# Sorting a unit's matmuls into a block of wide and a block of narrow ones

## The chip, the core and the metric

The program runs on one core of a Trainium2 chip. The metric is the device time of one execution in microseconds (us); lower is better. The chip's TensorE (PE in the profile) multiplies a stationary 128x128 block, loaded by an instruction of its own (PEld), with a moving operand of up to 512 columns and adds the product into PSUM. ScalarE (ACT), VectorE (DVE) and GpSimd (POOL) do the rest; SyncE (SP) issues most transfers.

## The reference, cut to what matters

Two transformer blocks over 256 tokens of width 2048. Block one: a gated convolution module, then a feed-forward part with a squared ReLU. Block two: stick-breaking and forgetting attention, 8 heads each, then another such feed-forward part. Everything is float32. The change touches the products that the reference writes as

```python
h @ w_up                                       # both feed-forward parts, 2048 -> 8192
proj = jnp.einsum('bsd,de->bse', h, w_in[l])   # of it the columns of q and k
```

## The kernel before, in words

**Hi and lo.** A float32 weight is split into `hi` (rounded to the matmul's fp32r format, by ACT, line 127) and `lo = raw - hi` (DVE, line 128). Activations are split in the same way; `xt[:, k, 0, :]` is the high half of 128 input columns for all 256 tokens, `xt[:, k, 1, :]` the low half. A product is the sum of hi·hi, hi·lo and lo·hi.

**Units.** All weights go through one list of steps. A unit is a piece of 512x512 weights (1 MB), loaded by SP into one of three `raw` buffers, split into one of three `hi` and one of three `lo` buffers, and used by one function. `emit` splits two units ahead (`SPLITS`) and loads three further ahead (`LOADS`), so the cast for unit i+2 is emitted before the matmuls of unit i; its buffers are those of unit i-1.

**The unit with stationary weights** (`ws_unit`, used by `up`, lines 614 to 632, and by q and k in `proj`). The weight block `wh` or `wl` is stationary. It holds 4 output blocks m by 4 input blocks k. For each (m, k) there is one wide matmul (`wh` with both halves of the activations, 512 columns, line 222) and one narrow matmul (`wl` with the high half alone, 256 columns, line 224, or 221 for the very last k). The two alternate, m outside and k inside. Four units kq = 0 to 3 add into the same four PSUM banks; they make a group of 64 wide and 64 narrow matmuls. Two PSUM tiles of two banks each, tag `ps2`, carry them: tile 0 for m = 0 and 1, tile 1 for m = 2 and 3. There are two `ps2` buffers in all.

**After kq = 3** each tile is read by an ACT copy and a DVE add (`u_t` line 626 and `u_z` line 628 for up; `q_t` lines 905 and 906 for q and k, where line 907 then writes `qk`). Only then may the next user of that tile start.

**The order around it.** Feed-forward: up(0), up(1), down(0), up(2), down(1) and so on; `down` is four units of `xs_unit`, in which the activations are stationary and every matmul is 512 wide (lines 231 to 233, tile `dn`, PSUM tag `ps1`). Mixer: for each of four groups of heads (two forgetting, two stick-breaking) v by `xs_unit` (tile `pv`, also `ps2`), q and k by `ws_unit` (tile `pj`), with the attention of the group before between the units: `z` products right after k, and `o` and `om` products between the next q units. After the first q comes the forget gate (`pf`). The first stage (tile `pw`, lines 518 to 521) uses 256-column matmuls only, each with its own load. From step 40 on, the instructions of each engine are ordered by the framework and not by hand.

Of the kernel before, what the change touches and what calls it, by code (L numbers as in the profile page):

```python
# [15 lines left out]
P = 128  # L16
T = 256
# [16 lines left out]
def kernel(  # L34
# [5 lines left out]
    x, out = x[0], out[0]  # L40
# [25 lines left out]

    state = {}

# [1 line left out]
    ident = const.tile([P, P], F32, name="ident")  # L70
    ones = const.tile([P, P], F32, name="ones")
    ones_c = const.tile([P, P], F32, name="ones_c")
# [17 lines left out]
        nc.scalar.dma_start(out=t, in_=bass.AP(tensor=v.tensor, offset=v.offset, ap=[[0, P], [1, D]]))  # L90
        return t

# [1 line left out]
    steps = []  # L94

    def unit_std(w, r0, c0):
# [76 lines left out]

    mm = nc.tensor.matmul

# [1 line left out]
    def split_act(src, hi, lo):  # L177
        nc.scalar.copy(hi, src)
        nc.vector.tensor_tensor(out=lo, in0=src, in1=hi.bitcast(F32), op=ALU.subtract)
# [31 lines left out]
    def new_ss(name):  # L211
        return small.tile([P, 2, 4], F32, tag="ss", name=name, bufs=2)

    def ws_unit(ps, hi, lo, xt, kq, m0=0, nm=4):
        for m in range(nm):
            for k in range(4):
                wh, wl = hi[:, k, m * P:(m + 1) * P], lo[:, k, m * P:(m + 1) * P]
                o = ps[m]
                last = kq == 3 and k == 3
                if last:  # L220
                    mm(o[:, 0:T], wl, xt[:, k, 0, :], start=False, stop=False, skip_group_check=True)
                mm(o, wh, xt[:, k, :, :], start=(kq == 0 and k == 0), stop=last)  # L222
                if not last:
                    mm(o[:, 0:T], wl, xt[:, k, 0, :], start=False, stop=False, skip_group_check=True)  # L224

    def xs_unit(ps, hi, lo, xt, first, last):
        for h in range(2):
# [4 lines left out]
                mm(ps[h], xh, lo[:, k, :], start=False, stop=False)  # L232
                mm(ps[h], xl, hi[:, k, :], start=False, stop=(last and k == 3))  # L233

# [1 line left out]
    s1 = ExitStack()  # L236
    p1 = s1.enter_context(tc.tile_pool(name="stage1", bufs=1))
    cpool = s1.enter_context(tc.tile_pool(name="cpool", bufs=4))
# [91 lines left out]
        for h in range(2):  # L330
            nc.gpsimd.tensor_tensor(out=res[:, h, :], in0=res[:, h, :], in1=rowbc, op=ALU.add)

# [1 line left out]
    xs_t = p1.tile([P, NB, T], F32, name="xs_t")  # L334
    u_t = [p1.tile([P, 2, T + 2 * PAD], F32, name=f"u{i}") for i in range(2)]
    acc0 = p1.tile([P, T], F32, name="acc0")
# [223 lines left out]
                            add_bias_rows()  # L560
                step(unit, fn)

# [1 line left out]
    def post_chunk(c, ss, gain, xts, delay):  # L564
        for h in range(2):
            sumsq(ss, h, c)

        def tr():
            xt = xt_tile("xn")
            for h in range(2):  # L570
                transpose_chunk(res[:, h, c * 512:(c + 1) * 512], h, c, gain, xt)
            xts.append(xt)
            if len(xts) == 4 and "after" in state:
                state.pop("after")()
        defer(delay, tr)
# [31 lines left out]
            srcs, _ = unit_std(w_pw2, q * 512, c * 512)  # L607
            step((srcs, "p" if q == 0 and c < 2 or (q, c) == (1, 0) else "v"), fn)

# [1 line left out]
    def ffn(w_u, w_d, tail):  # L611
        NG = FF // 512

        def up(g):
            for kq in range(4):
                def fn(hi, lo, kq=kq):
                    if kq == 0:
                        state["up"] = [ps2([P, 2, 512], f"up{i}") for i in range(2)]
                    pss = state["up"]
                    ws_unit([pss[m // 2][:, m % 2, :] for m in range(4)], hi, lo, state["xt"][kq], kq)  # L620
                    if kq == 3:
                        act = xt_tile("act")
                        for i in range(2):
                            ps = pss[i]
                            t = wk([P, 2, T], "u_t")
                            nc.scalar.copy(t, ps[:, :, T:2 * T])
                            z = wk([P, 2, T], "u_z")
                            nc.vector.tensor_tensor(out=z, in0=ps[:, :, 0:T], in1=t, op=ALU.add)
                            nc.vector.scalar_tensor_tensor(out=z, in0=z, scalar=0.0, in1=z, op0=ALU.max, op1=ALU.mult)
                            split_act(z, act[:, 2 * i:2 * i + 2, 0, :], act[:, 2 * i:2 * i + 2, 1, :])  # L630
                        state["act", g] = act
                step(unit_std(w_u, kq * 512, g * 512), fn)
# [59 lines left out]
            defer(2, spread)  # L692
        defer(1, rate)

# [1 line left out]
    s2 = ExitStack()  # L696

    def open_attention():
# [70 lines left out]
        state["lr"] = lr  # L769

    def attention(kind, grp, qk, v, mt):
        """Four heads: list of steps, each emitted in order with the projections between."""
        ap = state["ap"]
        qT, kT = qk
        per_pair = []
        for pair in range(2):
            st = {}
            heads = (2 * pair, 2 * pair + 1)
# [97 lines left out]
    def mixer():  # L876
        def proj(kind, grp, gi):
# [14 lines left out]
            for which in (0, 1):  # L892
                for kq in range(4):
                    def fn(hi, lo, kq=kq, which=which):
                        ap = state["ap"]
                        if kq == 0:
                            state["pj"] = [ps2([P, 2, 512], f"pj{i}") for i in range(2)]
                        pss = state["pj"]
                        ws_unit([pss[m // 2][:, m % 2, :] for m in range(4)], hi, lo, state["xt"][kq], kq)
                        if kq == 3:  # L900
                            dst = ap.tile([P, 4, T], F32, tag="qk", name=f"qk{which}", bufs=4)
                            rb = state["rb"][:, 1 - which:2 - which, :].to_broadcast([P, 2, T])
                            for i in range(2):
                                t = wk([P, 2, T], "q_t")
                                nc.scalar.copy(t, pss[i][:, :, T:2 * T])
                                nc.vector.tensor_tensor(out=t, in0=pss[i][:, :, 0:T], in1=t, op=ALU.add)  # L906
                                nc.vector.tensor_tensor(out=dst[:, 2 * i:2 * i + 2, :], in0=t, in1=rb, op=ALU.mult)
                            state["qk", gi, which] = dst
                            if which == 1:
                                mt = xt_tile("mt")  # L910
                                state["mt", gi] = mt
                                sts = attention(kind, grp, (state["qk", gi, 0], dst), state["v", gi], mt)
                                for n, s in enumerate(sts):
                                    defer(n + 1, s)
                    step(unit_std(w_in, kq * 512, base + 1024 * which + 512 * grp), fn)
                if gi == 0 and which == 0:
                    step(spread_gate, forget_gate)
# [54 lines left out]
                eng = nc.sync if j == 0 else nc.scalar  # L972
                eng.dma_start(out=out[h * P:(h + 1) * P, j * 1024:(j + 1) * 1024], in_=v)

# [1 line left out]
    for gi in range(len(groups)):  # L976
        stage1_group(gi)
    pw2()
# [54 lines left out]
```

## Time and profile before

| | |
|---|---|
| time, median of 3 runs | 2202.88 us (2202.71 to 2204.14) |
| span of the profiled execution, first to last instruction | 2200.8 us |
| PE busy | 2166.2 us, 98% of the span |
| DVE, ACT, POOL busy | 1436.8, 958.8, 175.2 us |
| mean granted TensorE clock | 0.996 of full speed |

The profiled execution has no time listed beside its span; the span is 2.1 us short of the median of the runs. "PE busy" counts modelled ends of pipelined matmuls, so the rate of a stream is read from start to start, not from the duration of one matmul.

### The profile page before, as it was taken

To read this page: it belongs to the slowest core of one execution; us is meant where nothing else is said; L and a number is where in the kernel's file an instruction comes from. 1 tells how busy PE (TensorE), PEld (TensorE's weight loads), DVE (VectorE), ACT (ScalarE), POOL (GpSimd) and SP (SyncE) were. 2 spreads that over 40 slices of the span, in tenths; PEclk is the share of its full clock that TensorE was granted. 3 is DMA by queue.
4 is the path that set the end of the run, shared out by engine and by line. 5 is a ranking of instruction groups with operands and counts; after the bars stand their busy time and mean duration, and the time that the engine had idled before them with its cause. 6 is when DMAs were issued, how large, how long until landed. Compare 5 with 4: busy or idle time off the path is not lost.

```text
span 2200.8 us, 27600 instructions
## 1 busy us (share of the span) xinstructions
PE 2166.2 (98%) x11521; PEld 1861.1 (85%) x11521; DVE 1436.8 (65%) x1648; ACT 958.8 (44%) x965; POOL 175.2 (8%) x88
## 2 busy tenths in 40 slices
PE   7999899999999999999999999999999999999998
PEld 7999778888888888888788888888888888888886
DVE  5997775666655666566866565676656665666656
ACT  6455454434333433343645454544333433343333
POOL 2886500000000000000000000000000000000000
PEclk9999999999999999999999999999999999999999
DMA  7555155555555555556544554455555555555553
GB/s 227 164 170 150 63 193 187 186 188 188 190 191 191 184 198 191 191 174 221 177 156 153 172 172 159 166 172 191 192 189 187 186 190 189 191 189 192 191 191 134
DMA packets 219612, 395.41 MB, mean 180 GB/s; under 512 B 8993, under 2 KB 46017, under 8 KB 219073
## 3 DMA queue, kind: packets, MB, share of 16 engines
q1 hardware_dynamic: 216160, 389.05, 54.6%
q10 hardware_dynamic: 2960, 4.27, 0.6%
q8 instruction: 90, 1.47, 0.3%
q0 software_dynamic: 368, 0.34, 0.1%
q14 instruction: 34, 0.28, 0.0%
HBM read 391.53 MB, written 2.10 MB: 179 GB/s over the span
## 4 chain that ended last, share of the span: by engine, by line
PE 97%; ACT 1%; DVE 1%; issue 0%; DMA 0%; ACTq 0%; SPq 0%; DVEq 0%
PE up L222 22%; PE dn L231 11%; PE dn L233 11%; PE dn L232 11%; PE up L224 10%; PE pj L222 5%; PE pj L224 3%; PE pw L521 2%; PE pw L518 2%; PE pw L520 2%; PE ca L386 2%; PE wo L232 1%; PE wo L233 1%; PE wo L231 1%; PE pv L233 1%; PE pv L231 1%
## 5 line engine op out<-in xcount | busy, mean ns | idle before, releaser
L128 DVE TENSOR_TENSOR lo<-raw,hi 128x2048 fp32r<-128x2048 f32 (+1 forms) x339 | 774.3, 2285 | 585.6 <-ACT hi L127 585.6
L127 ACT CAST hi<-raw 128x2048 fp32r<-128x2048 f32 (+1 forms) x369 | 702.8, 1906 | 935.9 <-PE up L222 340.3
L222 PE MATMUL up<-xn,hi 128*128 128x512 f32 x2048 | 718.3, 398 | 0.0
L224 PE MATMUL up<-xn,lo 128*128 128x256 f32 x1920 | 539.4, 281 | 0.0
L222 PEld LDWEIGHTS up<-xn,hi 128*128 128x128 f32 x2048 | 378.2, 188 | 83.8
L231 PE MATMUL dn<-hi,act 128*128 128x512 f32 x1024 | 398.8, 389 | 0.0
L233 PE MATMUL dn<-hi,act 128*128 128x512 f32 x1024 | 398.4, 389 | 0.0
L232 PE MATMUL dn<-lo,act 128*128 128x512 f32 x1024 | 398.3, 389 | 0.0
L224 PEld LDWEIGHTS up<-xn,lo 128*128 128x128 f32 x1920 | 362.5, 189 | 5.9
L641 DVE SCALAR_TENSOR_TENSOR res<-dn,rsq,res 128x512 f32<-128x512 f32 x256 | 191.4, 748 | 57.9 <-PE dn L233 57.9
L232 PEld LDWEIGHTS dn<-lo,act 128*128 128x128 f32 x1024 | 192.3, 188 | 40.1
L233 PEld LDWEIGHTS dn<-hi,act 128*128 128x128 f32 x1024 | 192.2, 188 | 40.1
L231 PEld LDWEIGHTS dn<-hi,act 128*128 128x128 f32 x1024 | 192.2, 188 | 38.6
L222 PE MATMUL pj<-xn,hi 128*128 128x512 f32 x512 | 179.7, 398 | 0.0
L394 DVE SCALAR_TENSOR_TENSOR acc<-u_p,wd,acc 128x256 f32<-128x256 f32 x385 | 151.6, 478 | 0.0
L128 POOL TENSOR_TENSOR lo<-raw,hi 128x2048 fp32r<-128x2048 f32 x30 | 138.5, 4620 | 85.6 <-ACT hi L127 85.6
L224 PE MATMUL pj<-xn,lo 128*128 128x256 f32 x480 | 134.5, 280 | 0.0
L518 PE MATMUL pw<-xa,hi 128*128 128x256 f32 x448 | 129.1, 288 | 0.7 <-ACT hi L127 0.7
L521 PE MATMUL pw<-xa,lo 128*128 128x256 f32 x448 | 127.6, 285 | 0.9 <-DVE lo L128 0.9
L520 PE MATMUL pw<-xa,hi 128*128 128x256 f32 x448 | 127.5, 285 | 0.0
L222 PEld LDWEIGHTS pj<-xn,hi 128*128 128x128 f32 x512 | 94.5, 188 | 20.6 <-DVE q_t L906 0.5
L224 PEld LDWEIGHTS pj<-xn,lo 128*128 128x128 f32 x480 | 90.6, 189 | 1.5
(259 smaller groups left out, 2033.5 us busy)
## 6 DMA issues: line engine op xcount, KB each, us to landing
raw<-in_ffn_w_up_dram SPq DMA_DIRECT2D x64, 1024.0 KB, 5.2
raw<-in_ffn_w_down_dram SPq DMA_DIRECT2D x64, 1024.0 KB, 5.1
raw<-in_w_up_dram SPq DMA_DIRECT2D x64, 1024.0 KB, 5.3
raw<-in_w_down_dram SPq DMA_DIRECT2D x64, 1024.0 KB, 5.0
raw<-in_w_in_dram SPq DMA_DIRECT2D x48, 1024.0 KB, 5.1
raw<-in_conv_w_pw_dram SPq DMA_DIRECT2D x64, 512.0 KB, 4.8
raw<-in_conv_w_pw_dram SPq DMA_DIRECT2D x16, 1024.0 KB, 5.1
raw<-in_w_out_dram SPq DMA_DIRECT2D x16, 1024.0 KB, 5.1
```

The source lines that it names most:

```text
L127: nc.scalar.copy(hi[:, j:j + n], raw[:, j:j + n])
L128: e.tensor_tensor(out=lo[:, j:j + n], in0=raw[:, j:j + n], in1=hi[:, j:j + n].bitcast(F32), op=ALU.subtract)
L222: mm(o, wh, xt[:, k, :, :], start=(kq == 0 and k == 0), stop=last)
L224: mm(o[:, 0:T], wl, xt[:, k, 0, :], start=False, stop=False, skip_group_check=True)
L231: mm(ps[h], xh, hi[:, k, :], start=(first and k == 0), stop=False)
L232: mm(ps[h], xh, lo[:, k, :], start=False, stop=False)
L233: mm(ps[h], xl, hi[:, k, :], start=False, stop=(last and k == 3))
L394: nc.vector.scalar_tensor_tensor(out=acc[k], in0=src, scalar=w, in1=acc[k], op0=ALU.mult, op1=ALU.add)
L518: mm(ps[:, m, :], wh, xt[:, k, 0, :], start=first and m % 2 == 0, stop=False, skip_group_check=True)
L520: mm(ps[:, m, :], wh, xt[:, k, 1, :], start=False, stop=False, skip_group_check=True)
L521: mm(ps[:, m, :], wl, xt[:, k, 0, :], start=False, stop=last, skip_group_check=True)
L641: nc.vector.scalar_tensor_tensor(out=r, in0=ps[h], scalar=state["rsq"][:, h:h + 1], in1=r, op0=ALU.mult, op1=ALU.add)
```

## The change

`ws_unit` issues the 16 wide matmuls of a unit in one block and the 16 narrow ones in another. For even kq the wide block comes first, for odd kq the narrow one, so that over a group the order is wide, narrow, narrow, wide, wide, narrow, narrow, wide. No matmul is added or taken away; the flags that begin and end an accumulation stay with the first and the last wide matmul of each m. The two unused parameters go. The rest of the diff takes out comments and a docstring.

```diff
-    def ws_unit(ps, hi, lo, xt, kq, m0=0, nm=4):
-        for m in range(nm):
-            for k in range(4):
-                wh, wl = hi[:, k, m * P:(m + 1) * P], lo[:, k, m * P:(m + 1) * P]
-                o = ps[m]
-                last = kq == 3 and k == 3
-                if last:
-                    mm(o[:, 0:T], wl, xt[:, k, 0, :], start=False, stop=False, skip_group_check=True)
-                mm(o, wh, xt[:, k, :, :], start=(kq == 0 and k == 0), stop=last)
-                if not last:
-                    mm(o[:, 0:T], wl, xt[:, k, 0, :], start=False, stop=False, skip_group_check=True)
+    def ws_unit(ps, hi, lo, xt, kq):
+
+        def wide():
+            for m in range(4):
+                for k in range(4):
+                    mm(ps[m], hi[:, k, m * P:(m + 1) * P], xt[:, k, :, :], start=(kq == 0 and k == 0),
+                       stop=(kq == 3 and k == 3), skip_group_check=True)
+
+        def narrow():
+            for m in range(4):
+                for k in range(4):
+                    mm(ps[m][:, 0:T], lo[:, k, m * P:(m + 1) * P], xt[:, k, 0, :], start=False, stop=False,
+                       skip_group_check=True)
+
+        for run in ((narrow, wide) if kq % 2 else (wide, narrow)):
+            run()
```

## Rows read from the trace of the kernel before

**Rows 1.** The page, busy time by engine, then the chain by engine and line.

```profile
PE 2166.2 (98%) x11521; PEld 1861.1 (85%) x11521; DVE 1436.8 (65%) x1648; ACT 958.8 (44%) x965; POOL 175.2 (8%) x88
...
PE 97%; ACT 1%; DVE 1%; issue 0%; DMA 0%; ACTq 0%; SPq 0%; DVEq 0%
PE up L222 22%; PE dn L231 11%; PE dn L233 11%; PE dn L232 11%; PE up L224 10%; PE pj L222 5%; PE pj L224 3%; PE pw L521 2%; PE pw L518 2%; PE pw L520 2%; PE ca L386 2%; PE wo L232 1%; PE wo L233 1%; PE wo L231 1%; PE pv L233 1%; PE pv L231 1%
```

**Rows 2.** The page, groups of instructions: the wide matmuls of up and pj.

```profile
L222 PE MATMUL up<-xn,hi 128*128 128x512 f32 x2048 | 718.3, 398 | 0.0
...
L222 PE MATMUL pj<-xn,hi 128*128 128x512 f32 x512 | 179.7, 398 | 0.0
```

**Rows 3.** Stretch, length, busy (x) of PE, PEld, DVE, ACT, clock, DMA, GB/s: up.

```profile
1003.96:1026.57 22.61, 22.60 (x128) 19.48 (x127) 0.68 (x1) 0.59 (x1) 1.00 0.59 188
```

**Rows 4.** The same, without ACT: the down group behind it, 96 starts, one overlap.

```profile
1026.57:1048.34 21.77, 21.77 (x97) 18.02 (x96) 5.24 (x7) 1.00 0.72 241
```

**Rows 5.** The same view: one pw group of the first stage, 256 columns only.

```profile
55.74:78.96 23.22, 23.22 (x192) 23.14 (x192) 0.99 (x2) 0.96 (x2) 1.00 0.59 190
```

**Rows 6.** Timeline of PE (start, duration): from down into up.

```profile
1003.74 0.39 PE L233 MATMUL dn<-hi,act 128*128 128x512 f32 x1
1003.97 0.39 PE L222 MATMUL up<-xn,hi 128*128 128x512 f32 x1
1004.19 0.28 PE L224 MATMUL up<-xn,lo 128*128 128x256 f32 x1
1004.30 0.40 PE L222 MATMUL up<-xn,hi 128*128 128x512 f32 x1
1004.54 0.28 PE L224 MATMUL up<-xn,lo 128*128 128x256 f32 x1
```

**Rows 7.** Timeline of PE: in kq = 3, two narrow, then two wide ones.

```profile
1021.86 0.28 PE L224 MATMUL up<-xn,lo 128*128 128x256 f32 x1
1021.98 0.28 PE L221 MATMUL up<-xn,lo 128*128 128x256 f32 x1
1022.10 0.63 PE L222 MATMUL up<-xn,hi 128*128 128x512 f32 x2
1022.57 0.28 PE L224 MATMUL up<-xn,lo 128*128 128x256 f32 x1
```

**Rows 8.** Timeline of PEld: a weight load of the first stage.

```profile
59.87 0.19 PEld L520 LDWEIGHTS pw<-xa,hi 128*128 128x128 f32 x1
```

**Rows 9.** Timeline of ACT and DVE: cast and subtraction of one unit.

```profile
998.77 1.91 ACT L127 CAST hi<-raw 128x2048 fp32r<-128x2048 f32 x1 [3.53 <-PE dn L233]
...
1000.71 2.29 DVE L128 TENSOR_TENSOR lo<-raw,hi 128x2048 fp32r<-128x2048 f32 x1 [1.24 <-ACT hi L127]
```

**Rows 10.** Timeline of ACT, DVE and PE: the seam from up(0) to up(1).

```profile
380.11 0.59 ACT L626 COPY u_t<-up 128x512 f32<-128x512 f32 x1 [1.01 <-PE up L222]
...
382.79 0.62 ACT L178 CAST act<-u_z 128x512 fp32r<-128x512 f32 x1 [2.09 <-DVE u_z L629]
383.31 0.58 ACT L626 COPY u_t<-up 128x512 f32<-128x512 f32 x1
...
381.34 0.69 DVE L628 TENSOR_TENSOR u_z<-up,u_t 128x512 f32<-128x512 f32 x1
382.06 0.69 DVE L629 SCALAR_TENSOR_TENSOR u_z<-u_z 128x512 f32<-128x512 f32 x1
...
384.05 0.68 DVE L628 TENSOR_TENSOR u_z<-up,u_t 128x512 f32<-128x512 f32 x1
...
382.50 0.63 PE L222 MATMUL up<-xn,hi 128*128 128x512 f32 x2
```

**Rows 11.** Timeline of ACT, DVE and PE: from k into z, first stick-breaking group.

```profile
1300.38 0.59 ACT L905 COPY q_t<-pj 128x512 f32<-128x512 f32 x1 [0.99 <-PE pj L222]
...
1302.35 0.69 DVE L907 TENSOR_TENSOR qk<-q_t,rb 128x512 f32<-128x512 f32 x1
...
1302.77 0.40 PE L222 MATMUL pj<-xn,hi 128*128 128x512 f32 x1
...
1303.24 0.59 PE L807 MATMUL z<-qk,qk 128*128 128x256 f32 x2
```

## The prediction, made before the changed kernel ran

> **What bounds the kernel now.** I read the page first: how busy each engine is, then the chain of work that ended last. PE is busy for 98% of the span and holds 97% of the chain; wide and narrow matmuls of up and pj alone are 40% of it [rows 1]. The reader is to see that only the rate at which PE takes matmuls counts, and that no other engine is above 65%. The granted clock is 1.00 in each stretch shown, the higher of its two levels, 2.4 GHz [rows 3 to 5], so there is no clock to win back.
>
> Then I read how long whole groups last from first start to next start, since the busy time of overlapping matmuls says nothing of their rate. One up group of 64 wide and 64 narrow matmuls takes 22.61 us [rows 3], 0.3533 us a pair; 28 of the 32 up groups take just that, the other four are the first two of each feed-forward part. The down group behind it, 96 wide ones, takes 21.77 us, 0.2268 us each [rows 4]. A pw group of 192 narrow ones takes 23.22 us, 0.1209 each [rows 5], with 0.120 as the median of 1,488 neighbouring starts inside such groups. So a wide one among wide ones and a narrow one among narrow ones cost 0.2268 + 0.120 = 0.3468 us, and alternating they cost 0.3533. The difference, 6.5 ns a pair, is what the change is about.
>
> **Does it hang on the neighbour or on the operands?** Down and pw move other tensors than up, so I looked for places where up itself leaves the alternation, in the timeline of PE. There are two. Behind a down group the first wide matmul of up follows wide ones, and it lasts 0.22 us to the next start, against 0.23 to 0.24 for those behind a narrow one [rows 6]; over the 31 complete places of this kind the median is 227 ns, against 236 in the alternation. And in kq = 3 the last k of each m is turned round: there two narrow ones meet, then two wide ones [rows 7]. The narrow ones lie 0.12 us apart, as in pw. The two wide ones take 0.47 us together, 0.235 each, so a wide one pays some 9 ns behind a narrow one and still 6 as second; the third is back at 227 ns by the starts of down behind up. The first narrow one behind wide ones takes 0.11 [rows 6], 7 ns less than 0.120. All four parts of the price are thus seen in this kernel's own operands, except a long wide run of up.
>
> **The change part by part.**
>
> *Blocks.* There are 2048 + 512 = 2560 pairs [rows 2], 40 groups (32 of up, 8 of q and k). 2560 x (0.3533 - 0.3468) = 16.6 us saved. Each group keeps two changes from narrow to wide (inside kq = 1 and kq = 3) and two from wide to narrow. A change to wide costs 2 x (0.235 - 0.2268) = 0.016 us, in all 40 x 2 x 0.016 = 1.3 us; a change to narrow gives back 0.007, in all 0.6 us. Net 15.9 us. With pw's 0.1209 in place of 0.120 it is 13.6 us; I take 0.120, since pw's group time holds its own seams.
>
> *Order within a unit.* A unit of odd kq now needs `lo` at its start, and one of even kq gives `hi` back 16 narrow matmuls (1.9 us) earlier. Both are free: the cast of a unit starts as its buffer falls free, two units ahead, and `lo` is there 4.23 us later (998.77 to 1003.00 [rows 9]), while two units take some 11 us. That leaves 6 us or more, and behind a casting ACT nothing waits longer than before. If this cover were gone, each of the 80 odd units would pay up to the subtraction's 2.29 us, 183 us in all; the 6 us exclude it. SP's loads go by the `raw` buffers, which the subtraction frees at the same time or up to 1.9 us earlier; with a DMA share of 0.6 to 0.7 [rows 3, 4] I cost that at nothing.
>
> *Seams, where the same PSUM tiles are wanted again at once.* In kq = 3 tile 0 used to be done half a unit (2.83 us) before the end; now its last wide one comes 8 x 0.227 = 1.81 us before it. The next unit wants tile 1 after 8 wide matmuls, 1.81 us, instead of 2.83. Three kinds of seam are hit:
>
> - up(0) to up(1), twice. ACT copy 0.59, DVE add 0.69, relu-square 0.69, cast 0.62, then the second copy and add: the second add ended at 384.73, 2.0 us after the group's end at 382.73 (the second of the two wide matmuls at 382.50), with the first copy begun 2.6 us ahead of it [rows 10]. Put 1.6 us ahead, and no longer held by the subtraction of a coming unit, the chain lets tile 1 go some 2.4 us after the end, 0.65 us late: 1.3 us for the two.
> - q to k without another unit between, in the last three head groups. The shorter chain (copy 0.59, add 0.69) fits: some 0.1 us each.
> - k to z, four times. z wants `qk` of the first two heads, written by copy, add and the multiply by `rb` (0.69): that now ends some 0.4 us behind k's last matmul; it ended at 1303.04, when k did, and z began at 1303.24 [rows 11]. Some 0.4 us for each stick-breaking group; the forgetting groups have two products that need no `qk` in front, 0.05 each.
>
> Together 2.5 us. Below it lies nothing (the framework may slip another matmul in between, as it did there); above it each of the nine seams pays a whole chain of 0.59 + 0.69 + 0.69 us, 18 us, which the copies that begin before the unit's end exclude in most.
>
> **Sum.** 15.9 - 2.5 = 13.4 us. The profiled span becomes 2200.8 - 13.4 = 2187.4 us; the median of the runs lies 2.1 us above the span, so 2202.9 - 13.4 = 2189.5 us.
>
> **Rivals.**
>
> *A wide run of up doesn't reach 227 ns (slower).* Long wide runs exist only in down, where the moving operand is a weight. If up's wide ones stayed at the 0.235 of rows 7, a group would take 64 x 0.235 + 64 x 0.120 = 22.72 us, and 40 x 0.11 + 2.5 = 7 us would be added: 2210 us. It decides from (22.61 - 64 x 0.120) / 64 = 0.2333 us on. For it speaks that the only neighbouring wide ones in up do cost 0.235; against it the 0.22 in rows 6. 6 in 100.
>
> *The narrow block becomes bound by its weight loads (slower).* Today each second load lies beside a wide matmul; then 32 follow each other beside narrow ones. One load is recorded with 0.19 us. At that spacing a group would take 64 x (0.2268 + 0.19) = 26.7 us, 163 us more in all, 2366 us; it decides from 0.126 us a narrow matmul on. Against it: in pw every narrow matmul has such a load of 0.19 us of its own [rows 8] and they come every 0.121 us [rows 5], so loads overlap. 2 in 100. The Trainium skill speaks for this rival (TensorE: Matmul & The Clock Gate, LDWEIGHTS): a load takes the block's columns over 1.2 GHz, an estimate of 107 ns for 128, about as long as a narrow matmul's own stream. By that figure the narrow block would just not be bound; pw's 0.121 us agrees.
>
> *The order is indifferent (no change).* Each matmul could carry a fixed cost that belongs to its operands: then the alternation costs what the sum of its parts costs, only the seams are left, and the time is 2202.9 + 2.5 = 2205.4 us, or 2203 without them. Rows 6 and 7 speak against it: the same line takes 0.22 or 0.235 us by what precedes it. 7 in 100. The Trainium skill states such a rule (the same page, Back-to-back issue gap): columns over 2.4 GHz plus 2.5 ns, an estimate of 216 + 109 = 325 ns a pair in any order. The trace has neither 325 nor one figure for both orders, so here I go by the rows.
>
> *The blocks come out mixed, or seams cost much more.* The framework orders the instructions; if it mixes blocks or stalls a seam by a whole chain, the gain is a part of 13.4 us: 2197 to 2202 us. The trace shows one such slip per seam, no more. 7 in 100.
>
> *More gain.* If narrow ones came at the 0.113 that the first one shows, 40 x 64 x 0.007 = 18 us more: 2171 us; 1,488 neighbours at 0.120 speak against it. 3 in 100.
>
> **How the numbers follow.** My forecast, 2189.5 us, has 75 in 100 and spans 2186 to 2197: pw's rate adds 2.3 us, seams -2.5 to +5. About 0.2% (4.4 us) is what a measurement of this kernel can tell from no change. Faster by more: the forecast, more gain and most of the mixed case, 84 in 100; within it: the indifferent order and a rest, 8; slower: the two slower rivals, 8. The range 2185.5 to 2197.5 us leaves out the rivals, which hold 2 in 10 with the faint ends of the forecast.
>
> **What would show it right or wrong.** An up group should last 22.2 us between starts, with 0.227 us in its wide blocks and 0.120 in its narrow ones; down groups should stay at 21.77. `up(1)` should start its third block m some 0.65 us late, and z of the stick-breaking groups 0.4 us. Wrong it is if wide starts in up lie 0.235 apart in the middle of a block, if narrow ones lie over 0.126 apart, or if PE waits for `lo`, `hi` or a load.

## The result and the profile after

The changed kernel takes 2189.91 us (median of 5 runs, 2189.72 to 2190.89) against 2203.1 us (5 runs, 2202.71 to 2204.14): ratio 0.9939, 95% interval 0.9927 to 0.9952. The forecast was 2189.5 us. Its profiled span is 2188.2 us, 12.6 us shorter than the one before. In the changed kernel line 219 is the wide and line 225 the narrow matmul; all later lines move down by 5.

The page, busy time by engine and chain by line; they answer to [rows 1]:

```profile
PE 2151.5 (98%) x11521; PEld 1862.8 (85%) x11521; DVE 1439.0 (66%) x1648; ACT 959.2 (44%) x965; POOL 175.2 (8%) x88
...
PE up L219 21%; PE up L225 11%; PE dn L236 11%; PE dn L238 11%; PE dn L237 11%; PE pj L219 5%; PE pw L526 2%; PE pw L523 2%; PE pw L525 2%; PE pj L225 2%; PE ca L391 2%; PE wo L238 1%; PE wo L237 1%; PE wo L236 1%; PE pv L238 1%; PE pv L237 1%
```

The same matmuls, the same bound: PE still sets the end. Next the stretches of one up group and of the down group behind it, with the columns of [rows 3, 4] (busy times of the instructions on `up`, then on `dn`, alone):

```profile
998.80:1021.02 22.22, 22.21 (x128) 19.50 (x127) 0.69 (x1) 0.59 (x1) 1.00 0.64 211
```

```profile
1021.03:1042.78 21.75, 21.74 (x96) 18.02 (x96) 5.23 (x7) 1.00 0.65 221
```

128 matmuls in 22.2 us where 22.61 stood, and down as it was. From start to start 30 of the 32 up groups take 22.23 us each; the first group of each feed-forward part, which has transposes between its matmuls, takes 23.24 and 23.25 us. The timeline of PE inside that group (x32 is a run):

```profile
1001.76 0.84 PE L219 MATMUL up<-xn,hi 128*128 128x512 f32 x3
1002.44 4.00 PE L225 MATMUL up<-xn,lo 128*128 128x256 f32 x32
1006.27 1.09 PE L219 MATMUL up<-xn,hi 128*128 128x512 f32 x4
```

32 narrow matmuls last (1006.27 - 1002.44) = 3.83 us, 0.120 each. Between neighbouring wide matmuls of up the median of the 1,952 spacings is 227 ns; the five behind a narrow block lie 233, 236, 228, 233 and 231 ns apart, then 227. The first two narrow ones take 113 and 119.

Where the time came from, by the first matmul of each stage (us, from the trace):

| stage | before | after | difference |
|---|---|---|---|
| to the first up | 355.46 | 355.29 | -0.17 |
| feed-forward 1, to the first q | 738.76 | 732.91 | -5.85 |
| mixer, to the second feed-forward part | 381.61 | 380.73 | -0.88 |
| feed-forward 2, to the last matmul | 710.68 | 704.59 | -6.09 |

These add up to 12.99 us; the program's very first matmul came 0.42 us later in the second trace. So the feed-forward parts gave 11.94 us, and 11.69 of it lies inside the up groups: 0.38 in each of thirty, 0.29 in the first of feed-forward 2 (23.54 before) and nothing in the first of feed-forward 1 (23.23 before). The mixer's 8 groups gave nothing: all runs of q and k matmuls together last 181.1 us in both traces.

Of the mixer's 0.88 us, 0.82 lie in the `z` products, 21.29 us before and 20.47 after. In a forgetting group each head has two products of `lr` over 32 rows of its own. Before, each came alone; while PE waits at the first of the stalls below, the framework now puts those of three heads side by side. PE before, then after:

```profile
1149.22 0.38 PE L786 MATMUL z<-lr 32*128 32x256 f32 x1
1149.44 0.28 PE L787 MATMUL z<-lr 32*128 32x256 f32 x1
```

```profile
1196.86 0.39 PE L791 MATMUL z<-lr 32*128 32x256 f32 x3
1197.09 0.28 PE L792 MATMUL z<-lr 32*128 32x256 f32 x3
```

The three start 7 ns apart and take 0.22 us together, as long as one took alone. No term of the forecast has this gain. What became of the one forecast for q and k is seen where PE waits.

In the last three groups of heads PE stands still at the start of k. DVE before the second of these stalls, then PE:

```profile
1266.75 2.29 DVE L128 TENSOR_TENSOR lo<-raw,hi 128x2048 fp32r<-128x2048 f32 x1
1268.96 0.68 DVE L869 TENSOR_TENSOR hr<-hr,ht 128x512 f32<-128x512 f32 x1
1269.68 0.88 DVE L872 SCALAR_TENSOR_TENSOR hl<-o,vt,hr 128x256 f32<-128x256 f32 x2
1270.48 0.68 DVE L866 TENSOR_TENSOR ht<-hr 128x512 f32<-128x512 f32 x1
1271.19 0.69 DVE L867 SCALAR_TENSOR_TENSOR ht<-om,ht 128x512 f32<-128x512 f32 x1
1271.80 0.68 DVE L179 TENSOR_TENSOR mt<-hl,mt 128x512 fp32r<-128x512 f32 x1
1272.40 0.42 DVE L868 TENSOR_SCALAR ht<-ht 128x512 f32<-128x512 f32 x1
1272.73 0.68 DVE L911 TENSOR_TENSOR q_t<-pj,q_t 128x512 f32<-128x512 f32 x1
...
1273.47 1.20 PE L219 MATMUL pj<-xn,hi 128*128 128x512 f32 x4 [0.79 <-DVE q_t L911]
```

DVE is full here: the subtraction for a coming unit, the tail of the norm step of the heads before, and only then the add that gives PSUM tile 0 back (line 911). The starts across this seam lie 1174 and 337 ns apart where the old kernel had 300 and 335. Over the three seams this is 0.31, 0.88 and 0.86 us more than before, 2.05 us.

The subtraction stands there because its cast came early. ACT before and after, the two casts whose subtractions stand around the norm step:

```profile
1268.44 1.91 ACT L127 CAST hi<-raw 128x2048 fp32r<-128x2048 f32 x1 [3.82 <-PE pj L222]
...
1274.55 1.91 ACT L127 CAST hi<-raw 128x2048 fp32r<-128x2048 f32 x1 [2.95 <-PE pj L222]
```

```profile
1260.66 1.91 ACT L127 CAST hi<-raw 128x2048 fp32r<-128x2048 f32 x1 [4.33 <-PE pj L219]
...
1264.78 1.91 ACT L127 CAST hi<-raw 128x2048 fp32r<-128x2048 f32 x1 [0.97 <-PE pj L219]
```

They were 6.1 us apart and are now 4.1: kq = 1 ends with its wide block and gives `hi` back at its end, kq = 2 ends with its narrow block and gives it back 1.9 us before.

### The profile page after: what moved, and what is told of

It reads as the page before. It is cut to its first block, busy times and chain, and to the rows that moved or that the text cites. A ratio compares the mean times of both kernels' runs of the same rounds, so it can differ in the third digit from the quotient of the medians.

```text
span 2188.2 us, 27599 instructions
## 1 busy us (share of the span) xinstructions
PE 2151.5 (98%) x11521; PEld 1862.8 (85%) x11521; DVE 1439.0 (66%) x1648; ACT 959.2 (44%) x965; POOL 175.2 (8%) x88
## 4 chain that ended last, share of the span: by engine, by line
PE 95%; DVE 2%; ACT 1%; issue 0%; DMA 0%; ACTq 0%; SPq 0%; DVEq 0%
PE up L219 21%; PE up L225 11%; PE dn L236 11%; PE dn L238 11%; PE dn L237 11%; PE pj L219 5%; PE pw L526 2%; PE pw L523 2%; PE pw L525 2%; PE pj L225 2%; PE ca L391 2%; PE wo L238 1%; PE wo L237 1%; PE wo L236 1%; PE pv L238 1%; PE pv L237 1%
## 5 line engine op out<-in xcount | busy, mean ns | idle before, releaser
L219 PE MATMUL up<-xn,hi 128*128 128x512 f32 x2048 | 482.3, 390 | 0.0
L225 PEld LDWEIGHTS up<-xn,lo 128*128 128x128 f32 x2048 | 254.2, 192 | 5.0
L225 PE MATMUL up<-xn,lo 128*128 128x256 f32 x2048 | 255.7, 283 | 0.0
L219 PE MATMUL pj<-xn,hi 128*128 128x512 f32 x512 | 122.4, 392 | 1.9 <-DVE q_t L911 1.9
L631 ACT COPY u_t<-up 128x512 f32<-128x512 f32 x64 | 37.7, 589 | 159.6 <-PE up L219 159.6
L633 DVE TENSOR_TENSOR u_z<-up,u_t 128x512 f32<-128x512 f32 x64 | 44.3, 692 | 77.7 <-ACT u_t L631 77.7
```

The costliest lines, as they stand in the source:

```text
L219: mm(ps[m], hi[:, k, m * P:(m + 1) * P], xt[:, k, :, :], start=(kq == 0 and k == 0), stop=(kq == 3 and k == 3), skip_group_check=True)
L225: mm(ps[m][:, 0:T], lo[:, k, m * P:(m + 1) * P], xt[:, k, 0, :], start=False, stop=False, skip_group_check=True)
```

## The experiments

The old kernel ran beside each: 2202.51 us (9 runs) for the other tile, the fixed order, tile by tile and up alone; 2204.47 us (one run) for the runs of two, of four or eight, and float32 ahead; 2203.06 us (9 runs) for the other three.

**A narrow matmul from the other tile.** Do neighbours of unlike width cost time, or neighbours that add into one bank?

```diff
+        else:
+            order = [e for j in range(16) for e in (("w", j), ("n", (j + 8) % 16))]
```

(kq = 0 and 3: blocks of 8 at the two ends, the same alternation between.)

> Alternates wide and narrow again, but a narrow matmul always adds into the other PSUM tile than the wide ones beside it (48 of 64 pairs of a group; the rest in blocks). If the price belongs to the change of width, an up group takes 22.23 + 0.75 x 0.38 = 22.5 us and the time is about 2201 us. If it belongs to two neighbours adding into the same bank, the group stays near 22.2 us and the time near 2190 us.

Measured: 2201.0 us (one run), 22.51 us a group. Alternating, the stream falls at once into 113, 232, 118, 241, 120, 236 ns, the old kernel's rhythm, while its two banks are different ones. So two neighbours in one bank are not what costs.

**Blocks in a fixed order.**

```diff
-        for run in ((narrow, wide) if kq % 2 else (wide, narrow)):
+        for run in (wide, narrow):
```

> Blocks without alternation, wide first in every unit: four changes from narrow to wide in a group where there are two. By the starts around a change (236 + 233 against 2 x 227, 113 + 119 against 2 x 120) one costs 7 ns, so 22.25 us a group and 0.6 us in all; the first tile of kq = 3 is then done only 0.96 us before the unit's end in place of 1.81, which puts some 2.5 us on the three seams from q to k: 2193 us. If the order of the blocks is worth nothing, 2190 us.

Measured: 2232.14 us (4 runs; ratio 1.0136, 1.0122 to 1.015). The groups are as expected, 22.24 us, but the seams are 42 us, not 2.5: nine of them cost 2.6 to 6.2 us each against the kernel of the next experiment, wait and slower matmuls behind it together. The one from up(0) to up(1), PE, ACT and DVE:

```profile
380.84 2.07 PE L225 MATMUL up<-xn,lo 128*128 128x256 f32 x16
385.95 6.25 PE L219 MATMUL up<-xn,hi 128*128 128x512 f32 x14 [3.04 <-DVE u_z L633]
...
381.04 1.91 ACT L127 CAST hi<-raw 128x2048 fp32r<-128x2048 f32 x1 [3.66 <-PE up L219]
382.85 1.06 ACT L631 COPY u_t<-up 128x512 f32<-128x512 f32 x2
...
383.00 2.29 DVE L128 TENSOR_TENSOR lo<-raw,hi 128x2048 fp32r<-128x2048 f32 x1 [3.27 <-ACT hi L127]
385.21 1.28 DVE L633 TENSOR_TENSOR u_z<-up,u_t 128x512 f32<-128x512 f32 x2
```

With its wide block first, kq = 3 gives its `hi` buffer back before the unit's end. The cast of a coming weight (381.04) goes ahead of the copy, its subtraction (383.00) ahead of the add, and PE waits 3.04 us for the add. A second price follows, seen in the stretch behind it (length, PE, PEld, DVE, ACT, POOL, granted clock, DMA, GB/s):

```profile
385.00:392.00 7.00, 6.05 (x14) 4.79 (x15) 3.99 (x7) 1.22 (x2) 0.00 (x0) 0.51 0.44 152
```

The granted clock is 0.51, the lower of its two levels, right after PE stood still: 14 wide matmuls in 6 us. PE's waits at the nine seams, 2.6 to 4.0 us each, add up to 28.6 us (10.8 for q to k, 8.7 and 3.0 for k to the next `ps2` tile, 6.1 for up). The rest of the 42 us goes with the lower clock behind them: in this trace it lasts 37.5 us in all, where the changed kernel has none between the end of the first stage (270 us) and its last few us.

**Narrow first in kq = 3 alone.** Is it alternation, or that one unit?

```diff
-        for run in ((narrow, wide) if kq % 2 else (wide, narrow)):
+        for run in ((narrow, wide) if kq == 3 else (wide, narrow)):
```

> Wide first in kq = 0 to 2, narrow first in kq = 3 alone. If the 42 us that the fixed order lost come from the last unit alone (with its narrow block at the end, the weight cast ahead of the next unit and its subtraction slip in front of the eviction), this kernel is at 2190 us like the changed one: 22.23 us a group plus one more change of 7 ns each, 0.3 us in all. If alternating the blocks matters in every unit, it stays well above, near 2200 us or more.

Measured: 2190.03 us (4 runs; ratio 0.9939, 0.9924 to 0.9954), 22.25 us a group. The whole 42 us is the order within the last unit. Alternating kq = 0 to 2 is worth 0.02 us an up group, and in the mixer it costs: 380.13 us here, 380.73 in the changed kernel. Here too kq = 2 ends with its narrow block, and yet k waits nowhere for the add. ACT, at the place of the second stall:

```profile
1260.54 1.91 ACT L127 CAST hi<-raw 128x2048 fp32r<-128x2048 f32 x1 [2.42 <-PE pj L219]
...
1266.55 1.91 ACT L127 CAST hi<-raw 128x2048 fp32r<-128x2048 f32 x1 [2.28 <-PE pj L219]
```

With kq = 1 ending in its narrow block as well, the two casts are 6.0 us apart, and the norm step of the first pair fits between their subtractions.

**q and k tile by tile at the seams.**

```diff
+        if by_tile and kq in (0, 3):
+            for ms in ((0, 1), (2, 3)):
+                for run in order:
+                    run(ms)
```

> For q and k alone, kq = 0 and kq = 3 are done tile by tile (wide and narrow of m = 0, 1, then of m = 2, 3). If the stalls from q to k come from the first tile being done late, they fall from 2.05 us over the old kernel's to about nothing, the added changes cost 0.1 us, and the time is 2188.0 us. If they come from VectorE, whose queue (subtraction, tail of the norm step) is full there, the time stays at 2189.9 us.

Measured: 2189.76 us (5 runs; ratio 0.9944, 0.9931 to 0.9956). Waits of k on the add: 1.8 us in the trace, 1.9 in the changed kernel's. Tile 0 done earlier doesn't help; the queue on DVE is what holds it.

**kq = 2 of q and k narrow first.** What puts the subtraction in front?

```diff
-        for run in ((narrow, wide) if kq % 2 else (wide, narrow)):
+        for run in ((narrow, wide) if kq % 2 or late and kq == 2 else (wide, narrow)):
```

> The changed kernel, with q and k in the order wide-narrow, narrow-wide, narrow-wide, narrow-wide. If the 0.94 us stalls from q to k come from kq = 2 giving its hi buffer back 1.9 us early, so that a subtraction of 2.29 us runs on VectorE before the adds, they fall to 0.3 us as in the old kernel and the time is 2188.2 us. If they come from elsewhere, 2189.9 us.

Measured: 2189.11 us (5 runs; ratio 0.9937, 0.9924 to 0.9949); the mixer lasts 380.10 us in the trace (380.73 in the changed kernel), and no wait of k on the add is left. DVE at the same place:

```profile
1266.63 0.69 DVE L869 TENSOR_TENSOR hr<-hr,ht 128x512 f32<-128x512 f32 x1
1267.36 0.88 DVE L872 SCALAR_TENSOR_TENSOR hl<-o,vt,hr 128x256 f32<-128x256 f32 x2
1268.55 2.29 DVE L128 TENSOR_TENSOR lo<-raw,hi 128x2048 fp32r<-128x2048 f32 x1 [0.31 <-ACT hi L127]
1270.76 0.69 DVE L179 TENSOR_TENSOR mt<-hl,mt 128x512 fp32r<-128x512 f32 x1
1271.36 0.69 DVE L866 TENSOR_TENSOR ht<-hr 128x512 f32<-128x512 f32 x1
1271.96 0.69 DVE L911 TENSOR_TENSOR q_t<-pj,q_t 128x512 f32<-128x512 f32 x1
```

The subtraction comes 1.8 us later, behind lines 869 and 872 of the first pair of heads, and the add now precedes the second pair's line 867 instead of following it. Together with narrow first in kq = 3 alone this shows the cause, and it is not kq = 2 by itself: the wait goes when kq = 2 gives `hi` back later, and also when kq = 1 gives it back earlier. In both the two casts are 6.0 us apart again, in place of 4.1. The runs of q and k fall to 179.9 us, but the `z` products take 0.4 us more than in the changed kernel. The 0.6 us that are left in the trace are below what the times of these runs can tell apart.

**Blocks for up alone.** `ws_unit` as changed for up, the old alternating loop for q and k.

> Blocks for up alone, q and k alternate as before. If the mixer's share of the change is eaten by its seams (five undisturbed q and k groups give 5 x 0.38 = 1.9 us, three groups of single units nothing, q to k takes back 2.05 us), the time is about 2189.9 us. If q and k give their 8 x 0.38 us in full, it is 2192.9 us.

Measured: 2191.55 us (5 runs, 2190.28 to 2192.18; ratio 0.995, 0.9936 to 0.9963). All five runs lie between the two expectations. In the trace the mixer takes 381.91 us, 1.2 us more than in the changed kernel and 0.3 more than before. Of the 1.2 us, 0.8 are the `z` products (21.29 against 20.47 us) and 0.3 the units of q and k (181.4 against 181.1): these themselves give almost nothing of their 3 us.

**Runs of two.**

```diff
+            for k in (0, 2):
+                for run in ((narrow, wide) if kq == 3 else (wide, narrow)):
+                    run(m, k)
+                    run(m, k + 1)
```

> Two wide, two narrow, and so on. If each change has the price seen at the block ends, four matmuls take 236 + 233 + 113 + 120 = 702 ns against 694 in blocks and 707 alternating: 22.46 us a group, and 2197 to 2199 us. If alternating has no price of its own and only settles into a bad phase, a rhythm of four could as well run at 694: 22.2 us a group and 2188 us (its seams are those of the old kernel).

Measured: 2190.99 us (one run), 22.29 us a group, 0.06 above whole blocks. Two wide and two narrow ones take 697 ns on the mean (234 + 236 + 116 + 112 and 232 + 231 + 114 + 118 in turn), not 702. A price for each change, taken from the ends of long blocks, doesn't hold.

**Runs of four or eight, within one m.**

```diff
+            narrow_first = kq == 3 or (kq > 0 and m % 2 == 0)
+            for run in ((narrow, wide) if narrow_first else (wide, narrow)):
+                for k in range(4):
+                    run(m, k)
```

> Runs of four or eight: blocks within one m, turned round where two of a kind can meet; 11 changes from narrow to wide in a group. At 7 ns each 22.30 us a group, 2.6 us more than with blocks over the unit, less about 1.9 us of seams: 2190.6 us. If a change costs more where runs are short, up to 16 ns, 22.4 us and 2194 us.

Measured: 2194.17 us (one run), 22.37 us a group: more than with runs of two, which have three times its changes. The number of changes is not the measure.

**Two float32 matmuls ahead of each alternating group.** The old kernel held a row that I had passed over. PE where a q unit follows the float32 products `o`:

```profile
1178.49 0.38 PE L846 MATMUL o<-pTs,v 128*128 128x128 f32 x2
1178.63 0.48 PE L222 MATMUL pj<-xn,hi 128*128 128x512 f32 x1
1178.95 0.28 PE L224 MATMUL pj<-xn,lo 128*128 128x256 f32 x1
1179.07 0.39 PE L222 MATMUL pj<-xn,hi 128*128 128x512 f32 x1
1179.30 0.28 PE L224 MATMUL pj<-xn,lo 128*128 128x256 f32 x1
1179.42 0.39 PE L222 MATMUL pj<-xn,hi 128*128 128x512 f32 x1
```

Behind a slow first start (0.32 us) a pair takes 0.35 us, in the raw starts 230 + 117 = 347 ns through the whole unit: alternating, at the rate of blocks. The old kernel's very first up group does the same behind its transposes, which the trace records as float32 matmuls too (two successive wide ones, 0.34 us apart):

```profile
361.30 0.60 PE L184 MATMUL pt<-ident,res 128*128 128x128 f32 x4
...
362.20 0.39 PE L222 MATMUL up<-xn,hi 128*128 128x512 f32 x1
...
362.54 0.39 PE L222 MATMUL up<-xn,hi 128*128 128x512 f32 x1
```

It keeps 347 ns a pair up to kq = 3, and it is the group that gained nothing by the change. The first group of feed-forward 2 has such transposes too, and behind the second four of them it ran at 353 ns; it gained 0.29 us.

```diff
     def ws_unit(ps, hi, lo, xt, kq, m0=0, nm=4):
+        if kq == 0:
+            for _ in range(2):
+                mm(ps[0][:, 0:P], ident, ident, start=True, stop=True, skip_group_check=True)
```

> The old kernel, alternating, with two float32 matmuls of 128 columns ahead of each group (their result is overwritten). In the old kernel the q and k units that follow float32 products alternate at 230 + 117 = 347 ns, all others at 353 on the mean. If the price of alternating is a phase that the stream falls into, and float32 matmuls ahead set it, groups alternate at 347 ns for kq = 0 to 2 at least: 22.3 us and some 0.25 us for what is added, about 2200 us. If alternating costs 353 whatever precedes it, 22.61 + 0.25 us a group and 2213 us.

Measured: 2209.87 us (one run), 22.72 us a group with what was added (0.36 us, and 0.09 on the first wide matmul). PE at the start of a group and at its third unit:

```profile
827.87 0.61 PE L217 MATMUL up<-ident 128*128 128x128 f32 x4
828.23 0.48 PE L225 MATMUL up<-xn,hi 128*128 128x512 f32 x1
828.55 0.28 PE L227 MATMUL up<-xn,lo 128*128 128x256 f32 x1
...
844.96 0.39 PE L225 MATMUL up<-xn,hi 128*128 128x512 f32 x1
845.19 0.28 PE L227 MATMUL up<-xn,lo 128*128 128x256 f32 x1
```

48 pairs on end run at 230 + 117 ns, until the first place in kq = 3 where two narrow ones meet; from there on it is 113, 233, 117, 241, 120, 236 again. So it is in 28 up groups and the first q group; the two up(1) and the first k group run a cycle of 231, 113, 232, 118 ns, also 347 a pair. But in the last six groups of q and k the same two matmuls stand ahead, and what follows them directly runs at 353 ns. One of these (two successive wide ones, 0.36 us apart):

```profile
1284.28 0.71 PE L217 MATMUL pj<-ident 128*128 128x128 f32 x4
...
1285.53 0.40 PE L225 MATMUL pj<-xn,hi 128*128 128x512 f32 x1
...
1285.89 0.40 PE L225 MATMUL pj<-xn,hi 128*128 128x512 f32 x1
```

Nor are float32 matmuls needed: in the old kernel the k group from 1280.6 us on has none in front, and three of its units run at 347 ns. What alternating costs is thus no price of a change of width. The stream has two steady rates, 347 and 353 ns a pair, and a stretch keeps the one that it falls into at its start until an irregular place; what in the start picks it is not shown. The time came out between the two expectations: what was added costs 0.45 us a group, not 0.25, kq = 3 falls back, and in six groups it doesn't set the faster rate.

**Blocks for up, runs of two for q and k.** `ws_unit` as changed for up, the loop of the runs of two for q and k.

> Blocks for up, runs of two for q and k. By the parts measured, up takes 711.8 us (blocks) and q and k 179.5 us (runs of two) in place of 181.1: 2188.3 us, faster than both kernels. If the runs of two owe their better seams to something in up, 2189.9 us.

Measured: 2188.9 us (5 runs, 2188.62 to 2190.01; ratio 0.9937, 0.9924 to 0.9949). q and k take 179.6 us, the mixer 379.99. By the trace it beats the changed kernel by 0.7 us in the mixer; by the times the two intervals overlap, since the stages before the first up alone vary by 1.6 us from trace to trace (355.07 to 356.72 us).

## Why the prediction was right, step by step

*The sum.* The 13.4 us came out at 13.0 in the trace, and that near only by luck: the feed-forward parts gave 11.94 us against 11.4 (12.7 less 1.3 for the seams), the mixer 0.88 against 2.0 (3.2 less 1.2), and 0.82 of the 0.88 are in `z` products that no term of the sum has.

*The rate.* Right: 227 and 120 ns in blocks, 22.23 us a group against some 22.2 forecast. A change to wide cost more than forecast, 26 ns over five matmuls in place of 16 over two. "No other engine is above 65%" leaves out the weight loads, 85% busy in [rows 1]; they did not become the limit, since 32 narrow matmuls with a load each came every 120 ns.

*Whose price it is.* Half right. It hangs on what precedes and not on the operands, as rows 6 and 7 were read; no rival of a slow wide run or a load-bound narrow block came true. But "a wide one pays some 9 ns behind a narrow one" was the wrong form of it. The old stream was in the slower of two rhythms; the same alternation ran at 347 ns in places of the old kernel already, and for 48 pairs in the experiment. Blocks help because they leave that rhythm, and the one up group that was out of it up to kq = 3 gained nothing. So the forecast's 0.40 us for each of the 40 groups was too much for the three q groups of single units: six of their twelve units, those behind `o`, already ran at 347 ns and went from 5.64 to 5.66 or 5.67 us.

*The seams.* The sum of 2.5 us was near (2.05 measured over the old kernel's) by luck, for each term was mis-sized. up(0) to up(1): 0.65 us each forecast, none measured. ACT and DVE there:

```profile
381.38 0.59 ACT L631 COPY u_t<-up 128x512 f32<-128x512 f32 x1 [3.77 <-PE up L219]
383.20 0.59 ACT L631 COPY u_t<-up 128x512 f32<-128x512 f32 x1 [1.22 <-PE up L219]
383.68 0.62 ACT L178 CAST act<-u_z 128x512 fp32r<-128x512 f32 x1
...
383.82 0.69 DVE L633 TENSOR_TENSOR u_z<-up,u_t 128x512 f32<-128x512 f32 x1 [0.40 <-ACT u_t L631]
```

The framework put the second copy ahead of the cast, which stood in front of it in [rows 10]. k to z: 0.9 us forecast for the four, no stall of PE on `qk` measured (its weight loads waited 0.9 us in all); in three of the four groups two matmuls of `pv` or `wo` had slipped in front. q to k: 0.1 each forecast, 0.31, 0.88 and 0.86 measured.

*Order within a unit.* No PE wait on `hi` or `lo` of q, k or up appeared, as forecast. The step that failed is "behind a casting ACT nothing waits longer than before": it weighed ACT and each unit's own cover, and not how close two casts come. At 4.1 us in place of 6.1 the second subtraction got ahead of the norm step on DVE, and the adds waited there. The kq = 2 experiment and the fixed order with the last unit turned show it for q to k, and the fixed order shows what it costs when it falls on the last unit: 42 us, a rival that the prediction did not name, one line away from this change.

Left open: why two rhythms exist, and what at the start of a stretch sets the faster one. Float32 matmuls ahead often go with it, but are neither enough nor needed; no experiment here varies only that.

## What to carry to other kernels

Read the rate of a matmul stream from start to start and compare it over all the places where the same line runs; two rhythms of one line show time to be had by order alone. When blocks are turned round, ask which buffer now falls free earlier, which queue its next filling enters and how close it comes to the filling before: the unit whose results are evicted next must give its cast buffer back last. Seams that are 0.1 to 0.7 us each in a hand-made sum came out at 0 to 0.9 by the framework's order, and at 2.6 to 6.2 us where a subtraction slips in front. A total that is right can hide two terms that are wrong: compare it stage by stage.

## What was not expected of the hardware

The same wide-narrow alternation runs steadily at 347 or at 353 ns a pair, for at least 48 pairs; one irregular place is enough to change from the faster to the slower, and the same two float32 matmuls ahead gave the faster in most groups and the slower in six. Three products over 32 rows each, in different rows, start 7 ns apart and take as long as one, 0.22 us. Runs of two come within 0.06 us a group of runs of 32. And PE standing still for 2.6 to 4.0 us is paid twice: the granted clock was 0.51 in the 7 us behind one such stall. The Trainium skill (TensorE: Matmul & The Clock Gate, Part 1) describes a gate that halves the clock of an idle array until it is busy again; the trace of the fixed order agrees.
